# Two-layer trunk: x fetched ahead of a weight chunk, loads moved from GpSimd's queue to SP's, and a planner's costs retuned

## The chip, the cores and the metric

One NeuronCore of a Trainium2 chip runs the whole program. The metric is the device time of one execution in microseconds; 0.2% is about 2.1 us here. Engines are TensorE (PE, with its weight loads PEld), VectorE (DVE), ScalarE (ACT), GpSimd (POOL) and SyncE (SP); SP, ACT and POOL each issue DMAs on a queue of their own.

## The reference

x has 512 tokens of width 1024, in float32. Two layers, each a token mixer and a SwiGLU network with RMS norms before and after:

```python
for i in range(DEPTH):                 # DEPTH = 2
    h = rmsnorm(x, norm_mix_pre[i])
    m = swa_sink_attention(h, ...) if i % 2 == 0 else chunked_sgu(h, ...)
    x = x + rmsnorm(m, norm_mix_post[i])
    h = rmsnorm(x, norm_ffn_pre[i])
    x = x + rmsnorm(swiglu(h, ffn_w_gate_up[i], ffn_w_down[i]), norm_ffn_post[i])
```

The attention has 16 query heads on 4 key heads of width 64, rotary positions, a window of 128 tokens and a learned sink per head. The width of the SwiGLU networks is 2816. Everything this document speaks of lies in the first layer's attention and at its two ends.

## The kernel before, in words

**Products.** Every float32 operand is split into a rounded high part and the remaining low part, and a product is made of three products of TensorE (high x high, high x low, low x high; `mm3`, line 281). Weights come in chunks of 128x1024 (512 KB). For a chunk, ScalarE rounds the high part `wh` (line 360), and the low part `wl` = `raw` - `wh` comes from VectorE's subtraction (line 331) or, for the chunks in `BY_DMA`, from ScalarE writing -`wh` (line 352) and an adding DMA on GpSimd's queue (line 355).

**The order of the work.** The kernel is recorded by a planner in Python. It keeps estimated clocks, `now[0]` for TensorE and `busy` for VectorE, ScalarE, the DMA queue and GpSimd; side tasks are generators (`Side`), and each yields the time at which its next step is due by these estimates. While the main loop records TensorE's products, every step that is due is recorded too. The estimates (`mm`, `V`, `A`, `ROT`, `RSD`, `DMA_LOW` and so on) therefore set only the order in which instructions stand on each engine. On the chip each engine runs its instructions in that order, and each waits for its real operands.

**DMAs.** The semaphores of SP's and ScalarE's DMAs are eight, used in turn: each DMA waits until the one eight places before it has landed. SP's queue is therefore a list with at most eight in flight, and what stands at its head holds up all that follows. At the start stand, in this order, chunk 0 of the weights, the transposed x in four pieces `xg0` to `xg3` with chunk 1 between the last two, chunk 2, x itself in four pieces `x0` to `x3` (`load_x`, line 453, called when chunk `NLATE` is due), then chunk 3, masks, tables (`cs`) and chunk 4. Chunks in `POOL_LOAD` go over GpSimd's queue.

**The start.** TensorE is kept busy with products of zeros (line 243) until `WARM`. The value projection (`vproj`, 96 products of 256 columns, 64 with the high parts of chunks 0 and 1 and then 32 with their low parts) needs the transposed x. The RMS norm of the first layer is applied late: `rows_rms` (line 1470) squares x0 to x3, takes the root and, by a diagonal matrix and one product with ones (line 1502), spreads it as `rbc`, with which the projections are multiplied as they leave PSUM.

**The attention.** Ten projection tiles follow, two pairs of key heads with one key tile and four query tiles each; each tile is 24 products of 512 columns on one chunk (chunks 2 to 11). `evac_qk` (line 982) takes a tile out of PSUM (line 997, into an `rt` tile), rotates it with four DMAs on SP's queue (line 1003), then does three VectorE steps (lines 1006, 1008, 1009), a ScalarE step for the high part (line 1013) and a VectorE step for the low part (line 1016). The planner takes `ROT` for the four DMAs. Scores come in units of one pair of heads and 128 queries, two groups of twelve products per unit (line 1088); the first group's first six products use the key and query 0, its second six the key and query 1. Then follow VectorE's maximum (line 1093), ScalarE's exponentials, the division by the sum (lines 1116 to 1126: VectorE scales all but `NA` of four score tiles, ScalarE the rest), transposes (line 1159) and the products with the values (line 1151). TensorE's rows of projections and, later, of the output projection (lines 1261 and 1280) stand between these as fillers.

**The end of the attention.** Each token block's output is squared, scaled and added to x (`Tok`, lines 621 to 666); `NextH` (line 512) then makes the transposed, normalised input of the SwiGLU network in parts `hh` (line 605) and `hl` (line 609), the first two blocks by a product with a diagonal matrix (line 590).

Of the kernel before, what the change touches and what calls it, by code (L numbers as in the profile page):

```python
# [13 lines left out]
P = 128  # L14
# [9 lines left out]
MAGIC = 0x5F3759DF  # L24
NW = 19
NP = 2
PITCH = 0.107
DMA_LOW = 6.0
BY_DMA = (8, 10, 12, 13, 14, 15, 16, 17, 18, 19, 20, 21, 22)
ROT = 4.0  # L30
NY = 3
P0 = 3
NT = 3
# [7 lines left out]
DLAT = 1.7  # L41
X_0 = 4.9
RS = (0.27406385, -4.2420223, 5.2654107, -0.90349173, 1.7067959)
RSD = 1.4
NA = 1
SCALE = ("av", "av", "av", "av")
DIAG = (0, 1)
POOL_LOW = ()
POOL_LOAD = range(5, 16)
ALT = (1, 2, 3)  # L50
WARM = 8.0
ORDER = ("w", 0, 1, 2, "w", 3)
ACT_SQ = ()
NLATE = 3
GROUPS = ((0,), (1,), (2, 3))


# [96 lines left out]
def trunk_kernel(ctx, tc, x_t, xt, w, cols, rows, ws_t, consts, out):  # L154
    nc = tc.nc
# [43 lines left out]
    now = [0.0]  # L199
# [74 lines left out]
    def mm(ps, a, b, start, stop):  # L274
        nc.tensor.matmul(ps, a, b, start=start, stop=stop)  # L275
        n = 1
        for d in b.shape[1:]:
            n *= d
        now[0] += max(n * 0.000422, PITCH)

    def mm3(ps, ah, al, bh, bl, start, stop):
        mm(ps, ah, bh, start, False)
# [11 lines left out]
    def fetch(free=0.0, most=NBLK):  # L294
        while len(raws) < min(NCH, most):
            c = len(raws)
            n = len(STREAM[c][0])
            if raw_used[0] + n > NRAW[stage[0] in (2, 6)] or used[0] + raw_used[0] + n > NW:
                return
            if c == NLATE:  # L300
                load_x()
            if c == NLATE + 1:
                nc.sync.dma_start(c_msk[:, 0:256], consts[:, 1024:1280])
                nc.sync.dma_start(c_msk[:, 256:384], consts[:, 1408:1536])
                nc.sync.dma_start(cs[:], consts[:, 0:1024])
                busy["d"] += 2.5
            tiles = []
            for b in reversed(STREAM[c][0]):
                raw = wp.tile([P, CB * P], F32, tag="w", name=nm("raw"))
                (nc.gpsimd if c in POOL_LOAD else nc.sync).dma_start(raw[:], w[b])  # L310
                busy["d"] = max(busy["d"], now[0], free) + 1.46
                tiles.insert(0, raw)
            raw_used[0] += len(tiles)
            raws[c] = (tiles, busy["d"] + DLAT)
# [117 lines left out]
    c_id = cp.tile([P, P], F32, name="c_id")  # L432
# [3 lines left out]
    xg = [wp.tile([P, 2, S], F32, tag="w", name=f"xg{q}") for q in range(NB)]  # L436
    used[0] += NB
    nc.scalar.dma_start(c_cols[:], cols)
    first_act = sp.tile([P, 8], F32, tag="first", name="first", bufs=1)
    nc.vector.memset(first_act[:], 0.0)  # L440
    nc.scalar.activation(first_act[:], first_act[:], AF.Copy)
    nc.gpsimd.dma_start(c_id[:], consts[:, 1280:1408])
    nc.gpsimd.dma_start(c_row[:], rows[0:272].partition_broadcast(P))
    arrive = {}
    busy["d"] = X_0 - DLAT + 0.2 - 1.46
    for o in ORDER:
# [65 lines left out]
    class NextH:  # L512
# [57 lines left out]
        def turn(self, ts):  # L570
            if self.h is None:
                self.h = [[hp.tile([P, S], F32R, tag=t, name=nm(t)) for _ in range(KT)] for t in ("hh", "hl")]
            n = P * len(ts)
# [3 lines left out]
            for k0 in range(0, KT, kn):  # L577
# [7 lines left out]
                for k in range(k0, k0 + kn):  # L585
                    for i, t in enumerate(ts):
# [3 lines left out]
                            nc.tensor.matmul(dst, xs[t][:, k * P:(k + 1) * P], self.src[t], start=True, stop=True)  # L590
                        else:
                            nc.tensor.transpose(dst, self.src[t][k // 4][:, (k % 4) * P:(k % 4 + 1) * P], ident)  # L592
                        now[0] += 0.22 if self.diag(t) else 0.11
                if 1 in ts and k0 + kn == KT and self.dg is not None:
                    give("rt")
                Side(self.evac(ts, range(k0, k0 + kn), ps, now[0] + 0.2, alt), now[0] + 0.2, True)
# [375 lines left out]
    def attention(nx_in, g1o, nx_out):  # L972
# [132 lines left out]
        def softmax(u, g2, st, es, sm, f):  # L1105
# [9 lines left out]
            yield f  # L1115
            nc.vector.tensor_tensor(sm[:, jj], sm[:, jj], es[:, jj], ALU.add)
            nc.vector.reciprocal(sm[:, jj], sm[:, jj])
            V(4, f, 0.13)
            V(4, f, 0.15)
            f = busy["v"] + LAT  # L1120
            for j in js[NA:]:
                nc.vector.tensor_scalar(p(j), p(j), sm[:, j:j + 1], None, ALU.mult)
# [7 lines left out]
        def values(u):  # L1130
# [13 lines left out]
            def pv(kt):  # L1144
# [4 lines left out]
                for i in range(2):  # L1149
                    o = (2 * pr + i) * 64  # L1150
                    nc.tensor.matmul(po[i * 64:i * 64 + 64, :], vt[n - nkt + 1 + kt][:, o:o + 64], todo[2 * kt + i],  # L1151
                                     start=kt == 0, stop=kt == nkt - 1)
                    now[0] += 0.02 if i else 0.86
                    give("t")

            for z, (i, kt) in enumerate(groups):
# [462 lines left out]
```

## Time and profile before

| | |
|---|---|
| median of 3 runs | 1044.04 us (1043.73 to 1044.79) |
| the profiled execution | 1043.52 us |
| its span, first to last instruction | 1041.7 us |
| mean granted clock of TensorE | 0.995 |
| busy: PE, DVE, ACT, POOL | 1024.0, 665.8, 453.1, 35.3 us |

A line such as `PE acc L275 <- ACT ga L1013: 4.2, 1, 4.2` in the table of waits says who waited (engine, tile, line of the kernel), for whom, how long in total, how often and how long at most. A line of the timeline begins with start and duration in us; in brackets stands the engine's idle time before the instruction and what ended it. A line of the stretches gives, for each engine, the busy time and the number of instructions, then the granted clock, the DMA share and GB/s. A line of a group has, after its count, busy us and the mean in ns of one instruction, then the idle time before them. TensorE's products overlap, so what one costs is the distance from start to start, not its duration.

### The profile page before, as it was taken

The page shows a single profiled execution, that of the slowest core. Times are in us where ns is not written, and L with a number is a line of the kernel's source. Part 1 is how long each engine was busy: PE and PEld are TensorE (multiplying, and loading weights), DVE is VectorE, ACT ScalarE, POOL GpSimd, SP SyncE. Part 2 cuts the span into 40 slices and gives each one's busy share as a digit, 9 for nine tenths or more (in the row PEclk, how much of TensorE's full clock was granted, in tenths as well). Part 3 has the DMA queues.
Part 4 walks back from the last instruction along what each step waited for, and adds up shares of the span by engine and source line. Part 5 has one row for each costly group of instructions (what it writes and reads, how often), then busy time and mean ns, then how long its engine had stood idle before and what let it go on. Part 6 is the DMA issues. An engine that isn't in the chain of part 4 may idle for free.

```text
span 1041.7 us, 13505 instructions
## 1 busy us (share of the span) xinstructions
PE 1024.0 (98%) x5137; PEld 850.4 (82%) x5137; DVE 665.8 (64%) x1209; ACT 453.1 (43%) x791; POOL 35.3 (3%) x43
## 2 busy tenths in 40 slices
PE   8989999999999999999999999999999999999997
PEld 7766666988888888888889888899888888888886
DVE  5679877644445658778594967474344656787746
ACT  5349886532233333344264343563223334334421
POOL 1101002000000000000010000110000000000000
PEclk9989999999999999999999999999999999999999
DMA  9456555143435455554243332033444544555302
GB/s 349 116 147 162 133 139 165 42 133 130 162 131 190 144 162 184 208 173 161 83 142 104 99 126 78 24 139 122 146 137 168 196 142 156 187 198 186 123 20 81
DMA packets 42961, 148.11 MB, mean 142 GB/s; under 512 B 5344, under 2 KB 5856, under 8 KB 42896
## 3 DMA queue, kind: packets, MB, share of 16 engines
q1 hardware_dynamic: 38640, 133.52, 38.4%
q0 software_dynamic: 3536, 12.79, 5.4%
q8 instruction: 40, 0.66, 0.3%
q10 hardware_dynamic: 720, 0.94, 0.3%
q14 instruction: 25, 0.20, 0.1%
HBM read 135.69 MB, written 2.10 MB: 132 GB/s over the span
## 4 chain that ended last, share of the span: by engine, by line
PE 89%; DMA 4%; DVE 4%; ACT 1%; SPq 1%; issue 1%; DVEq 0%; ACTq 0%
PE acc L275 86%; DMA rt<-rt 2%; DMA raw<-w 1%; DMA x<-x_t 1%; PE acc L1151 1%; PE aux L1159 1%; SPq L1003 1%; PE aux L592 1%; DMA c_cols<-cols 0%; DVE rt L1006 0%; DVE rt L1008 0%; DVE p L1093 0%; DVE wl L331 0%; DVE rt L1009 0%; DVE rt L997 0%
## 5 line engine op out<-in xcount | busy, mean ns | idle before, releaser
L275 PE MATMUL acc<-hh,wh 128*128 128x512 f32 (+1 forms) x960 | 353.1, 368 | 0.0
L275 PE MATMUL acc<-hl,wh 128*128 128x512 f32 (+1 forms) x960 | 350.7, 365 | 2.1 <-DVE hl L609 2.1
L275 PE MATMUL acc<-hh,wl 128*128 128x512 f32 (+1 forms) x960 | 350.4, 365 | 0.0
L331 DVE TENSOR_TENSOR wl<-raw,wh 128x1024 fp32r<-128x1024 f32 x187 | 228.0, 1227 | 149.7 <-ACT wh L360 79.4
L275 PEld LDWEIGHTS acc<-hl,wh 128*128 128x128 f32 x960 | 181.7, 189 | 31.3 <-DVE hl L609 2.6
L275 PEld LDWEIGHTS acc<-hh,wh 128*128 128x128 f32 x960 | 181.6, 189 | 29.6 <-issue 0.2
L275 PEld LDWEIGHTS acc<-hh,wl 128*128 128x128 f32 x960 | 181.5, 189 | 28.9
L360 ACT ACTIVATE wh<-raw 128x1024 fp32r<-128x1024 f32 x160 | 165.7, 1052 | 90.6 <-PE acc L275 57.6
L275 PE MATMUL acc<-wh,rt 128*128 128x512 f32 x496 | 162.3, 389 | 0.0
L275 PE MATMUL acc<-wh,ga 128*128 128x512 f32 (+1 forms) x344 | 120.0, 396 | 0.0
L275 PEld LDWEIGHTS acc<-wh,rt 128*128 128x128 f32 x496 | 93.1, 188 | 19.4
L275 PE MATMUL acc<-wl,rt 128*128 128x512 f32 x248 | 96.5, 389 | 0.0
L891 DVE TENSOR_TENSOR m<-m,acc 128x512 f32<-128x512 f32 x80 | 51.9, 684 | 44.2 <-PE acc L275 32.9
L275 PEld LDWEIGHTS acc<-wh,ga 128*128 128x128 f32 x344 | 64.4, 188 | 18.6 <-issue 4.1
L275 PE MATMUL acc<-wl,ga 128*128 128x512 f32 (+1 forms) x206 | 79.1, 384 | 0.0
L338 ACT ACTIVATE wh<-raw 128x1024 fp32r<-128x1024 f32 x40 | 42.3, 1059 | 71.9 <-DVE raw L343 71.9
L869 ACT ACTIVATE rt<-t 128x512 fp32r<-128x512 f32 x40 | 25.3, 633 | 87.1 <-DVE t L864 68.9
L275 PEld LDWEIGHTS acc<-wl,rt 128*128 128x128 f32 x248 | 46.6, 188 | 9.6
L343 DVE TENSOR_TENSOR raw<-raw,raw 128x1024 f32<-128x1024 f32 x40 | 48.8, 1219 | 0.0
L778 ACT ACTIVATE t<-acc 128x512 f32<-128x512 f32 (+1 forms) x38 | 20.2, 531 | 59.6 <-PE acc L275 59.6
L636 POOL TENSOR_TENSOR m<-m,row 128x512 f32<-128x512 f32 x12 | 16.8, 1430 | 846.6 <-ACT acc L502 846.6
L275 PEld LDWEIGHTS acc<-wl,ga 128*128 128x128 f32 x206 | 38.8, 189 | 6.2
(151 smaller groups left out, 967.6 us busy)
## 6 DMA issues: line engine op xcount, KB each, us to landing
raw<-w SPq DMA_DIRECT2D x229, 512.0 KB, 3.5
wl<-raw POOLq DMA_DIRECT2D x13, 512.0 KB, 5.2
raw<-w POOLq DMA_DIRECT2D x11, 512.0 KB, 7.1
row<-rows SPq DMA_DIRECT2D x8, 512.0 KB, 4.8
rt<-rt SPq DMA_DIRECT2D x40, 64.0 KB, 3.0
xg<-xt SPq DMA_DIRECT2D x4, 512.0 KB, 8.5
x<-x_t SPq DMA_DIRECT2D x4, 512.0 KB, 13.4
out<-x SPq DMA_DIRECT2D x4, 256.0 KB, 2.1
```

The source lines that it names most:

```text
L275: nc.tensor.matmul(ps, a, b, start=start, stop=stop)
L331: nc.vector.tensor_tensor(wl[:], raw[:], wh[:].bitcast(F32), ALU.subtract)
L338: nc.scalar.activation(wh[:], raw[:], AF.Copy)
L343: nc.vector.tensor_tensor(raw[:], raw[:], tiles[1][:], op)
L360: nc.scalar.activation(wh[:], raw[:], AF.Copy)
L592: nc.tensor.transpose(dst, self.src[t][k // 4][:, (k % 4) * P:(k % 4 + 1) * P], ident)
L636: nc.gpsimd.tensor_tensor(self.m[c][:], self.m[c][:], self.g1[:, cols2[c]], ALU.mult)
L778: nc.scalar.activation(t1[:, hf], pg[:, hf], AF.Silu)
L869: nc.scalar.activation(hi, src, AF.Copy)
L891: nc.vector.tensor_tensor(d, d, ps[i][:], ALU.subtract if sign == "-" else ALU.add)
L1003: nc.sync.dma_start(ro[o:o + 32, hf], t1[q * 32:q * 32 + 32, hf])
L1151: nc.tensor.matmul(po[i * 64:i * 64 + 64, :], vt[n - nkt + 1 + kt][:, o:o + 64], todo[2 * kt + i], start=kt == 0, stop=kt == nkt - 1)
```

## The change

Line numbers after it are one lower, but for lines 302 to 437, which are the same. Its parts:

- `BY_DMA` loses chunks 8 and 10: their low parts come from VectorE's subtraction (line 331) instead of ScalarE's step and the adding DMA.
- `NLATE` 3 to 2: x0 to x3 stand ahead of chunk 2 on SP's queue, and chunk 3 and all behind it follow.
- `POOL_LOAD` 5..15 to 8..15: chunks 5, 6 and 7 go over SP's queue.
- `c_row` (value bias and sinks) goes from GpSimd's queue at the start to SP's queue behind chunk 2; the identity `c_id` goes from GpSimd's queue to ScalarE's.
- `NA` 1 to 0: VectorE scales all four score tiles of a group, ScalarE none.
- `WARM` 8.0 to 7.3: 34 products of zeros instead of 37.
- Estimates: `ROT` 4 to 6, `RSD` 1.4 to 1.0, the cost of a product by columns, of products with 64 rows, of transposes with a diagonal, of the reciprocal and of a values product.

```diff
-PITCH = 0.107
-BY_DMA = (8, 10, 12, 13, 14, 15, 16, 17, 18, 19, 20, 21, 22)
-ROT = 4.0
+BY_DMA = (12, 13, 14, 15, 16, 17, 18, 19, 20, 21, 22)
+ROT = 6.0
-RSD = 1.4
-NA = 1
+RSD = 1.0
+NA = 0
-POOL_LOAD = range(5, 16)
+POOL_LOAD = range(8, 16)
-WARM = 8.0
+WARM = 7.3
-NLATE = 3
+NLATE = 2
...
-        now[0] += max(n * 0.000422, PITCH)
+        now[0] += 0.058 if a.shape[0] == 64 else max(n * 0.0004168 + 0.0136, 0.112)
...
             if c == NLATE + 1:
+                nc.sync.dma_start(c_row[:], rows[0:272].partition_broadcast(P))
                 nc.sync.dma_start(c_msk[:, 0:256], consts[:, 1024:1280])
...
     nc.scalar.dma_start(c_cols[:], cols)
+    nc.scalar.dma_start(c_id[:], consts[:, 1280:1408])
...
-    nc.gpsimd.dma_start(c_id[:], consts[:, 1280:1408])
-    nc.gpsimd.dma_start(c_row[:], rows[0:272].partition_broadcast(P))
...
-                        now[0] += 0.22 if self.diag(t) else 0.11
+                        now[0] += 0.11
...
-            V(4, f, 0.13)
-            V(4, f, 0.15)
+            V(4, f, 0.18)
+            V(4, f, 0.2)
...
-                    now[0] += 0.02 if i else 0.86
+                    now[0] += 0.02 if i else 0.71
```

The order of the instructions changes on every engine through the attention. Three places matter for what follows. The first is the start of SP's queue; `raw_32` is chunk 2, `raw_35` chunk 3, `raw_40` chunk 4 before, and `raw_59`, `raw_63`, `raw_66`, `raw_71` are chunks 4 to 7 after. Before:

```order
L310 DMA raw_2_111<-w 128x1024
L450 DMA xg3_99<-xt 128x1024
L310 DMA raw_32_179<-w 128x1024
L455 DMA x0_87<-x_t 128x1024
L455 DMA x1_88<-x_t 128x1024
L455 DMA x2_89<-x_t 128x1024
L455 DMA x3_90<-x_t 128x1024
L310 DMA raw_35_241<-w 128x1024
L303 DMA c_msk_92<-consts 128x256
L304 DMA c_msk_92<-consts 128x128
L305 DMA cs_95<-consts 128x1024
L310 DMA raw_40_290<-w 128x1024
```

And after, from x on:

```order
L454 DMA x3_90<-x_t 128x1024
L310 DMA raw_32_182<-w 128x1024
L302 DMA c_row_94<-rows 128x272
L303 DMA c_msk_92<-consts 128x256
L304 DMA c_msk_92<-consts 128x128
L305 DMA cs_95<-consts 128x1024
L310 DMA raw_35_242<-w 128x1024
L310 DMA raw_59_358<-w 128x1024
L310 DMA raw_63_384<-w 128x1024
L310 DMA raw_66_399<-w 128x1024
L310 DMA raw_71_427<-w 128x1024
L1002 DMA rt_67_404<-rt_67_404 32x512 x4
```

Chunk 2 stands behind x0 to x3 now, c_row comes in, and the first rotation (`rt_67`) stands behind chunk 7.

The second place is VectorE's row around the rotation of query 1, the third tile (`rt_80` before, `rt_83` after; the key is `rt_66` or `rt_67`, query 0 `rt_74` or `rt_75`, query 2 `rt_87` or `rt_91`). Before:

```order
L331 TENSOR_TENSOR wl_78_473<-raw_71_433,wh_77_472 128x1024
L1006 SCALAR_TENSOR_TENSOR rt_74_447<-rt_74_447,c_cols_91,cs_95 128x512
L1008 SCALAR_TENSOR_TENSOR rt_74_447<-rt_74_447,c_cols_91,cs_95 128x512
L1009 TENSOR_TENSOR rt_74_447<-rt_74_447 128x512
L997 TENSOR_TENSOR rt_80_495<-acc_75_448,rbc_396 128x512
L1016 TENSOR_TENSOR ga_5_118<-rt_74_447,ga_4_117 128x512
L331 TENSOR_TENSOR wl_86_536<-raw_79_484,wh_85_535 128x1024
L997 TENSOR_TENSOR rt_87_538<-acc_81_496,rbc_396 128x512
L1006 SCALAR_TENSOR_TENSOR rt_80_495<-rt_80_495,c_cols_91,cs_95 128x512
```

After, where `wl_81` and `wl_89` are the low parts of chunks 8 and 10:

```order
L331 TENSOR_TENSOR wl_81_490<-raw_74_442,wh_80_489 128x1024
L996 TENSOR_TENSOR rt_83_495<-acc_76_448,rbc_366 128x512
L1005 SCALAR_TENSOR_TENSOR rt_75_447<-rt_75_447,c_cols_91,cs_95 128x512
L1007 SCALAR_TENSOR_TENSOR rt_75_447<-rt_75_447,c_cols_91,cs_95 128x512
L1008 TENSOR_TENSOR rt_75_447<-rt_75_447 128x512
L331 TENSOR_TENSOR wl_86_521<-raw_79_473,wh_85_520 128x1024
L1015 TENSOR_TENSOR ga_5_117<-rt_75_447,ga_4_116 128x512
L331 TENSOR_TENSOR wl_89_538<-raw_82_493,wh_88_537 128x1024
L996 TENSOR_TENSOR rt_91_543<-acc_84_496,rbc_366 128x512
L1005 SCALAR_TENSOR_TENSOR rt_83_495<-rt_83_495,c_cols_91,cs_95 128x512
```

The evacuation of query 1 has moved from behind the three steps of query 0 to ahead of them, and more stands between it and its own first step.

The third place is VectorE's row at the end of the attention, where the last four of eight `hl` pieces of the first two token blocks are made. Before (between `hl_337` and the first update of x3 stand the eight steps of a root):

```order
L642 TENSOR_TENSOR m_253_1615<-m_253_1615,row_254_1617 128x512
L609 SCALAR_TENSOR_TENSOR hl_336_1941<-aux_358_2008,c_cols_91,hh_328_1933 128x256
L609 SCALAR_TENSOR_TENSOR hl_337_1942<-aux_358_2008,c_cols_91,hh_329_1934 128x256
L508 SCALAR_TENSOR_TENSOR u_360_2036<-sq_310_1881 128x1
...
L655 SCALAR_TENSOR_TENSOR x3_90<-m_243_1552,rc_366_2043,x3_90 128x512
L655 SCALAR_TENSOR_TENSOR x3_90<-m_253_1615,rc_366_2043,x3_90 128x512
L609 SCALAR_TENSOR_TENSOR hl_338_1943<-aux_359_2017,c_cols_91,hh_330_1935 128x256
L609 SCALAR_TENSOR_TENSOR hl_339_1944<-aux_359_2017,c_cols_91,hh_331_1936 128x256
```

After:

```order
L331 TENSOR_TENSOR wl_356_1995<-raw_298_1818,wh_355_1994 128x1024
L608 SCALAR_TENSOR_TENSOR hl_333_1930<-aux_357_2000,c_cols_91,hh_325_1922 128x256
L608 SCALAR_TENSOR_TENSOR hl_334_1931<-aux_357_2000,c_cols_91,hh_326_1923 128x256
L608 SCALAR_TENSOR_TENSOR hl_335_1932<-aux_358_2008,c_cols_91,hh_327_1924 128x256
L608 SCALAR_TENSOR_TENSOR hl_336_1933<-aux_358_2008,c_cols_91,hh_328_1925 128x256
L331 TENSOR_TENSOR wl_363_2049<-raw_309_1870,wh_362_2048 128x1024
L641 TENSOR_TENSOR m_257_1599<-m_257_1599,row_258_1601 128x512
L507 SCALAR_TENSOR_TENSOR u_368_2083<-sq_310_1876 128x1
```

The last two pieces have moved ahead of the root and of the updates of x3; a chunk's low part stands ahead of the four.

## The prediction

> **What bounds the kernel now.** I read the page first, then TensorE's waits over the whole span, then the timeline and the stretches around the largest wait, and last the chain of waits that leads to it.
>
> ```profile
> span 1041.7 us, 13505 instructions
> PE 1024.0 (98%) x5137; PEld 850.4 (82%) x5137; DVE 665.8 (64%) x1209; ACT 453.1 (43%) x791; POOL 35.3 (3%) x43
> ...
> PE acc L275 <- ACT ga L1013: 4.2, 1, 4.2
> PE acc L275 <- DVE hl L609: 2.1, 2, 1.4
> ...
> PE aux L590 <- issue: 0.9, 1, 0.9
> PE aux L1159 <- ACT t L1163: 0.3, 1, 0.3
> ```
>
> TensorE is busy 98% of the span, so only two things can move the time: work of TensorE, which this change leaves alone but for three warming products, and TensorE's gaps, 17.7 us in all. The waits name the largest: one of 4.2 us for a rotated query (line 1013). Here it is on TensorE's timeline (start, duration), with the granted clock of the stretches around it (PEclk, third column from the right) and of the rest of the attention:
>
> ```profile
> 51.01 0.55 PE L275 MATMUL acc<-gb,ga 64*128 64x128 f32 x6
> 55.79 1.20 PE L275 MATMUL acc<-gb,ga 64*128 64x128 f32 x6 [4.22 <-ACT ga L1013]
> 56.92 0.79 PE L275 MATMUL acc<-hh,wh 128*128 128x512 f32 x1
> ...
> 61.35 0.42 PE L275 MATMUL acc<-hl,wh 128*128 128x512 f32 x1
> ...
> 54.00:55.00 1.00, 0.00 (x0) 0.00 (x0) 0.97 (x2) 0.00 (x0) 0.00 (x0) 0.78 0.90 348
> 55.00:61.00 6.00, 5.17 (x16) 4.00 (x17) 4.59 (x15) 3.20 (x11) 0.00 (x0) 0.50 0.50 153
> ...
> 62.00:174.00 112.00, 111.40 (x637) 77.77 (x635) 87.81 (x296) 88.48 (x238) 17.14 (x19) 1.00 0.58 140
> ```
>
> Half of the first scores run at 51.01, the other half at 55.79. After about 3 us of standing still the granted clock falls to 0.50. Six score products then take 1.13 us (55.79 to 56.92) instead of 0.55, and ten projection products 4.43 us (56.92 to 61.35) where ten at full clock take 2.27 (0.227 each, worked out below). The wait thus costs 4.22 + 0.58 + 2.16 = 7.0 us.
>
> The Trainium skill (TensorE: Matmul & The Clock Gate, Part 1: The HAM clock gate) gives about 3.4 us of standing still before the clock halves and about 3.4 us of work before it is back. Its fall agrees with the row; by its return the slow part would cost half of 3.4, 1.7 us, and the wait 5.9. The rows show some 6.5 us at half clock, so 7.0 stands.
>
> What TensorE waits for, on the chain of work (start, duration), and from the GpSimd queue's timeline:
>
> ```profile
> 46.22 0.61 DVE rt L997
> ...
> 48.67 4.14 DMA rt<-rt
> ...
> 52.93 0.75 DVE rt L1006
> ...
> 55.10 0.64 ACT ga L1013
> ...
> 48.27 0.89 POOL L355 DMA_DIRECT2D wl<-raw  x1 [13.53 <-ACT wl L352]
> ```
>
> The third rotation (query 1) leaves PSUM only at 46.22. Its four DMAs take until 52.93, 6.1 us after 46.83; the last meets the adding DMA of chunk 8, issued at 48.27. Three VectorE steps follow (52.93 to 55.10, 2.2 us) and ScalarE's high part (0.64).
>
> **The start.** ScalarE's first steps show when transfers land (they start on landing), TensorE's rows what they hold up:
>
> ```profile
> 9.03 1.34 ACT L1461 ACTIVATE hh<-xg,c_cols 128x512 fp32r<-128x512 f32 x2 [1.47 <-DMA xg<-xt]
> 11.80 1.34 ACT L1461 ACTIVATE hh<-xg,c_cols 128x512 fp32r<-128x512 f32 x2 [1.43 <-DMA xg<-xt]
> ...
> 14.52 1.34 ACT L1461 ACTIVATE hh<-xg,c_cols 128x512 fp32r<-128x512 f32 x2 [0.22 <-DMA xg<-xt]
> 15.80 1.06 ACT L360 ACTIVATE wh<-raw 128x1024 fp32r<-128x1024 f32 x1
> 17.08 0.64 ACT L1483 ACTIVATE j<-x 128x512 f32<-128x512 f32 x1 [0.22 <-DMA x<-x_t]
> ...
> 20.60 0.64 ACT L1483 ACTIVATE j<-x 128x512 f32<-128x512 f32 x1 [1.51 <-DMA x<-x_t]
> ...
> 22.82 0.63 ACT L1483 ACTIVATE j<-x 128x512 f32<-128x512 f32 x1 [1.50 <-DMA x<-x_t]
> ```
>
> ```profile
> 7.81 0.36 PE L275 MATMUL acc<-wh,hh 128*128 128x256 f32 x1
> ...
> 14.35 0.39 PE L275 MATMUL acc<-wh,hh 128*128 128x256 f32 x1 [1.69 <-ACT wh L360]
> ...
> 18.28 4.00 PE L275 MATMUL acc<-wl,hh 128*128 128x256 f32 x32
> 22.12 0.40 PE L275 MATMUL acc<-hh,wh 128*128 128x512 f32 x1
> ...
> 26.24 1.02 PE L1502 MATMUL aux<-rt,ones 128*128 128x512 f32 x2
> ...
> 27.34 0.40 PE L275 MATMUL acc<-hl,wh 128*128 128x512 f32 x1
> ...
> 50.69 0.39 PE L275 MATMUL acc<-hh,wl 128*128 128x512 f32 x1
> ```
>
> A 512 KB transfer takes 1.28 us when SP's queue is alone (14.52, 15.80, 17.08), 2.2 us (20.60 to 22.82) when chunks 6 and 7 come over GpSimd's queue beside it, and 2.8 us (9.03 to 11.80) with chunk 5 and c_row there. The change keeps that queue free until the value projection has ended. The products of the value projection take 0.12 us (32 of them from 18.28 to 22.12); 96 would take 11.5 us, and from 7.81 to 22.12 they took 14.3. So 2.8 us are waits, 1.69 of them for chunk 1. A projection product takes 0.227 us (103 from 27.34 to 50.69).
>
> After, in steps of 1.28 us from xg1's predecessor (about 6.2, one ScalarE pair, 1.34, and its idle 1.47 before 9.03): xg1 7.5, xg2 8.8, chunk 1 10.1, xg3 11.3, x0 to x3 12.6 to 16.5, chunk 2 17.7, c_row 18.1. Chunk 1's high part (1.06) is there at 11.2, before its first product (7.81 + 32 x 0.12 = 11.7), so 2.4 of the 2.8 us go; the rest I leave to VectorE's last low parts. Three warming products fewer are worth 0 to 0.5; I take 0.1. The value projection ends at 19.6. The product with ones comes 3.4 us after x3 (22.82 to 26.24): 19.9. With its neighbour it holds TensorE 1.1 us (26.24 to 27.34), 0.87 beyond that neighbour. The low part of chunk 2 (a 1.2 us VectorE step behind the diagonal and the nsink step, which now needs c_row) is there at 21.1, when the third product of the first tile needs it. So the projections start at 20.8 instead of 22.12 + 0.87 = 23.0: **-2.2 us**, between -2.8 and -0.5 (chunk 2 late by 1.7).
>
> **The first scores.** There stand 123 projection products ahead of them, before and after: the larger ROT does not move them on TensorE. What moves is VectorE's row: the evacuation of query 1 stood behind the three steps of query 0 and now stands ahead of them. Their DMAs meet loads on GpSimd's queue as before, but no adding DMA of chunk 8 or 10. Rotations, from evacuation to the step behind, first and slowest:
>
> ```profile
> 31.98 0.68 DVE L997 TENSOR_TENSOR rt<-acc,rbc 128x512 f32<-128x512 f32 x1
> ...
> 39.16 0.75 DVE L1006 SCALAR_TENSOR_TENSOR rt<-rt,c_cols,cs 128x512 f32<-128x512 f32 x1 [4.35 <-DMA rt<-rt]
> ...
> 64.11 0.70 DVE rt L997
> ...
> 67.61 5.97 DMA rt<-rt
> ```
>
> That is 6.5 us, and 8.8 us (64.81 to 73.58). After: the key's tile ends at 20.8 + 24 x 0.227 = 26.2, leaves by 26.9, is rotated by 33.4 (6.5) and through the three steps by 35.6. Two low parts (1.2 each), its own low part and query 1's evacuation (0.7 each) bring that to 39.4. With 6.1 us again it is rotated at 45.5, when VectorE has done its other 6.0 us (three steps, two low parts, two of 0.7). High part at 48.3, low part behind one more chunk at 49.6. The first six scores come at 51.01 - 2.2 = 48.8, the second six, which read query 1, at 49.3 and its low part at 49.7. The wait goes: **-6.7 us**, leaving 0.3 for so thin a margin. Next late would be the same low part. With 8.8 us for both rotations the wait is 4.0 us and the clock falls again: -0.2 is the other bound. Rotations stay behind chunks 4 to 7 on SP's queue; query 0's four DMAs wait for exactly those to land. Behind c_row come six transfers of 512 KB and two small ones: at 1.28 us each they end near 26, at 2.2 near 32, when query 0's tile ends too (20.8 + 48 x 0.227 = 31.7). That is hidden, barely in the second case.
>
> **VectorE's added work.** Steps and means in the attention:
>
> ```profile
> L1122 DVE TENSOR_SCALAR p<-p,sm 128x256 f32<-128x256 f32 (+1 forms) x36 | 9.9, 333 | 0.4
> L331 DVE TENSOR_TENSOR wl<-raw,wh 128x1024 fp32r<-128x1024 f32 x8 | 9.8, 1220 | 3.3 <-ACT wh L360 3.3
> ...
> L1126 ACT ACTIVATE p<-p,sm 128x256 f32<-128x256 f32 (+1 forms) x12 | 5.6, 463 | 0.7 <-DVE sm L1117 0.5
> ```
>
> Sixteen scalings, one of four in two groups of eight units, come from ScalarE (12 of them in this row) to VectorE (0.333 each, 5.3 us), and two low parts (2.4 us). VectorE has 24 us free from 62 to 174 and TensorE waited there only 0.3 us, for a link of the same chain; I double that: **+0.6 us**, between 0 and 5.3. Two ScalarE copies and two adding DMAs go, at nothing, since nothing waits for them but the rotation above.
>
> **The end of the attention.** The longer of the two waits for hl is for its last pieces:
>
> ```profile
> 186.69 0.87 DVE L609 SCALAR_TENSOR_TENSOR hl<-aux,c_cols,hh 128x256 fp32r<-128x256 f32 x2
> ```
>
> These stood behind the last token's chain and now stand ahead of it, behind one chunk. Of 1.4 us I take **-1.0 us**, between -2.1 (both waits) and 0 (a step behind becomes late); the 0.9 us stay. The retuned costs of one product change little else: TensorE's waits, asked for the first 200 us alone, are the same rows, so the rest has none to lose.
>
> **The sum.** -2.2 - 6.7 + 0.6 - 1.0 = -9.3. The profiled execution took 1043.5 us (span 1041.7), 0.5 below the median: 1034.2 + 0.5 = **1034.7 us**. All bounds at their best give -2.8 - 7.0 - 2.1 = -11.9, 1032.1.
>
> **Rivals.**
> - *A rotation is late again* (the first scores, or a later one: 8.8 us is on record). For: the margin is under 1 us. Against: no adding DMA beside it. A wait of 2 to 4 us, with or without the halved clock: 1037 to 1041.5. Chance 0.21.
> - *SP's queue stays at 2.2 us a transfer.* x3 lands at 6.2 + 8 x 2.2 = 23.8, chunk 2 at 26.0, its low part (1.06 + 1.2) at 28.3; TensorE stands from 19.6 and the clock halves: the projections start 5.3 us later instead of 2.2 earlier, with up to 2.1 more for the clock, and the rest gives 7.1 back: 1042 to 1044. Against: GpSimd's queue is empty then. Chance 0.05.
> - *VectorE becomes the bound of the attention* (the slower case). While TensorE stood and crawled, VectorE caught up; if it sets the stage, the 7.0 us are no gain and 7.7 us come on top: 1044.0 - 2.2 + 7.7 = 1049.5. It decides once VectorE has no idle left; from 62 to 174 it is busy 87.81 of 112 us, 78%. Chance 0.05.
> - *The added scalings hold back GpSimd's queue.* Eleven adding DMAs remain; each late by one more scaling (0.333) is 3.7 us if TensorE waits for all: 1038.4. Against: none of TensorE's waits names a weight's low part from such a DMA. Chance 0.03. By the Trainium skill (SBUF — State Buffer, SBUF: two separate sides) a VectorE step that uses both read ports keeps GpSimd from writing its DMA descriptors; no run here shows it.
> - The change not doing what it says: the order has both subtractions on VectorE, so none.
>
> **Chances.** The forecast has 0.66, from 1031.8 to 1037. The range 1031.8 to 1041 leaves out the slower case and parts of two rivals. About 0.2% (2.1 us) is what a measurement of this kernel can tell from no change: faster 0.88 (the forecast, nearly all of the late rotation, the scalings), same 0.07 (SP's slow queue and what is left of a late rotation), slower 0.05.
>
> **What would show it.** Right: chunk 1's wait gone and the first projection at about 20.8; the first scores at about 49 in one piece with the clock at 1.00 from 50 to 62; the last hl pieces without a wait. Wrong: a wait for line 1012's ScalarE step with a clock of 0.50 behind it, a wait for chunk 2 near 20, or new waits between 75 and 145 behind VectorE's scalings.

## The result and the profile after

The changed kernel takes 1037.27 us (median of 4 runs, 1037.13 to 1037.39), the kernel before 1043.9 us (1043.73 to 1044.79) on the same chip: a ratio of 0.9934, with a 95% interval of 0.9923 to 0.9946. That is 6.6 us faster where 9.3 were forecast; the time lies 2.6 us above the 1034.7 of the forecast, inside the range (1031.8 to 1041) and 0.3 us outside the 1031.8 to 1037 that the forecast itself was given. The profiled execution took 1037.27 us (before 1043.52).

The page of the changed kernel, and then TensorE's largest waits over the span (who waited, for whom, total, times, longest):

```profile
span 1035.5 us, 13502 instructions
...
PE 1019.8 (98%) x5134; PEld 847.8 (82%) x5134; DVE 669.7 (65%) x1227; ACT 447.1 (43%) x773; POOL 30.3 (3%) x36
```

```profile
PE aux L591 <- ACT m L557: 2.9, 5, 1.3
PE aux L1158 <- ACT t L1162: 2.0, 2, 1.0
PE aux L589 <- issue: 1.7, 1, 1.7
```

The waits that the change aimed at are gone: chunk 1's (1.7), the rotated query's (4.2) and the two for hl (2.1). Three others are longer or new, and the largest stands in no row of before: transposes (line 591) that wait five times for ScalarE's line 557. It lies behind 500 us, in a part that the prediction gave no term. There `NextH` makes the input of the next network: the root of each token block's mean square (nine small VectorE steps from line 542 on), then x times the root, half by VectorE (line 560), half by ScalarE (line 557), then the transposes.

**The first 60 us went as forecast.** TensorE's timeline of the changed kernel (start, duration): the ones product, the third projection product, the twelve first scores and the two products that answer to 56.92 and 61.35 of before:

```profile
19.52 1.10 PE L1501 MATMUL aux<-rt,ones 128*128 128x512 f32 x2 [0.20 <-DVE rt L1497]
...
21.32 0.50 PE L274 MATMUL acc<-hh,wl 128*128 128x512 f32 x1 [0.24 <-DVE wl L331]
...
48.97 0.89 PE L274 MATMUL acc<-gb,ga 64*128 64x128 f32 x12
49.78 0.50 PE L274 MATMUL acc<-hh,wh 128*128 128x512 f32 x1
...
52.16 0.39 PE L274 MATMUL acc<-hl,wh 128*128 128x512 f32 x1
```

The stretch that stood at half clock before:

```profile
55.00:61.00 6.00, 6.00 (x28) 4.96 (x27) 4.80 (x8) 3.82 (x5) 1.41 (x2) 1.00 0.79 201
```

The first scores begin at 48.97 instead of 51.01, all twelve in one piece, and the clock stays at 1.00. The eleventh product behind them stands at 52.16, before at 61.35: 9.2 us earlier.

**Where the rest went.** The same VectorE steps in both kernels show how far the whole is ahead. First before: the first step of a root near 520, the update of x near 667. Then the same steps after:

```profile
524.72 0.16 DVE L543 SCALAR_TENSOR_TENSOR u<-s 128x2 f32<-128x2 f32 x1 [0.19 <-ACT m L502]
...
667.50 1.41 DVE L655 SCALAR_TENSOR_TENSOR x<-m,rc,x 128x512 f32<-128x512 f32 x2
```

```profile
514.29 0.16 DVE L542 SCALAR_TENSOR_TENSOR u<-s 128x2 f32<-128x2 f32 x1 [0.19 <-ACT m L501]
...
658.96 1.42 DVE L654 SCALAR_TENSOR_TENSOR x<-m,rc,x 128x512 f32<-128x512 f32 x2
```

And TensorE's last product, before and after:

```profile
1034.36 0.28 PE L275 MATMUL acc<-wh,gb 128*128 128x256 f32 x1
```

```profile
1027.89 0.28 PE L274 MATMUL acc<-wh,gb 128*128 128x256 f32 x1
```

The changed kernel is 10.4 us ahead at 514, more than forecast, 8.5 at 659, and 6.5 at the end. It gained 10.4 us in the first 200 us and lost 3.9 at the two places where the next network's input is made. The first of these places on TensorE, before and after:

```profile
528.59 0.60 PE L592 MATMUL aux<-c_id,m 128*128 128x128 f32 x4
```

```profile
515.90 0.39 PE L274 MATMUL acc<-wh,gb 128*128 128x512 f32 x1
517.56 0.33 PE L591 MATMUL aux<-c_id,m 128*128 128x128 f32 x1 [1.28 <-ACT m L557]
518.18 0.55 PE L591 MATMUL aux<-c_id,m 128*128 128x128 f32 x3 [0.28 <-ACT m L557]
```

ScalarE's scaling in the kernel before:

```profile
527.21 1.34 ACT L558 ACTIVATE m<-x,rc 128x512 f32<-128x512 f32 x2 [1.91 <-DVE rc L497]
```

Before, that pair ended at 528.55, 0.04 us ahead of the transposes, which began 3.87 us behind the root's first step (524.72 to 528.59) and did not wait; nothing was spare. After, TensorE arrives at about 516.1, 1.8 us behind that step (514.29), and stands. In TensorE's row the transposes have moved ahead of nine products; nine products of 0.227 us are the 2.0 us. The root takes 2.4 us here in both kernels (514.29 to 516.69 after), because one of its steps takes 1.21 us beside a scaling on GpSimd (last section); the planner took it as 1.7 before and as 1.3 after, which fits a root that is not held (165.13 to 166.47 in `lo_pool`) and not this one.

### The profile page after: what moved, and what is told of

It reads as the page before. It is cut to its first block, busy times and chain, and to the rows that moved or that the text cites. A ratio compares the mean times of both kernels' runs of the same rounds, so it can differ in the third digit from the quotient of the medians.

```text
span 1035.5 us, 13502 instructions
## 1 busy us (share of the span) xinstructions
PE 1019.8 (98%) x5134; PEld 847.8 (82%) x5134; DVE 669.7 (65%) x1227; ACT 447.1 (43%) x773; POOL 30.3 (3%) x36
## 4 chain that ended last, share of the span: by engine, by line
PE 92%; ACT 3%; DVE 2%; DMA 2%; issue 0%; SPq 0%; DVEq 0%; ACTq 0%
PE acc L274 89%; PE acc L1150 1%; PE aux L1158 1%; DMA raw<-w 1%; PE aux L591 1%; DMA xg<-xt 1%; ACT m L501 0%; ACT m L557 0%; ACT p L1112 0%; PE aux L589 0%; DVE wl L331 0%; ACT wh L360 0%; DVE x L654 0%; ACT acc L501 0%; DVE m L641 0%
```

## Theories

*Order*: the two retuned estimates that hold beyond the attention, a root (`RSD` 1.4 to 1.0) and a product (0.216 to 0.227 us for 512 columns), make the planner call for the transposes too early. A shorter root makes them due sooner, and a longer product puts fewer products into the same estimated time. In the order of the instructions the root's estimate alone moves the first transposes ahead of 6 products, the product's alone of 3, both of 9; no run times the two apart. *Chain* (rival): the root and the scaling themselves come later in the changed kernel, so that any order would wait.

For the first scores there were two candidates as well: the place of query 1's evacuation in VectorE's row, or the adding DMA of chunk 8 that runs beside its rotation. The later runs take the best kernel so far, `late_old`, and undo or move one thing each.

## The experiments

| kernel | median us | ratio to before, 95% interval |
|---|---|---|
| late_old | 1033.26 | 0.9892 (0.9878 to 0.9905) |
| late_new | 1048.18 | 1.0036 (1.0023 to 1.0048) |
| start_only | 1047.19 | 1.0028 (1.0018 to 1.0039) |
| rot_only | 1050.27 | 1.0055 (1.0042 to 1.0067) |
| lo_bydma | 1042.52 | 0.9983 (0.9974 to 0.9991) |
| lo_rot4 | 1038.91 | 0.9943 (0.9929 to 0.9956) |
| lo_na1 | 1040.66 | 0.9961 (0.9949 to 0.9973) |
| lo_mmold | 1038.08 | 0.9939 (0.9927 to 0.9950) |
| lo_diag | 1037.63 | 0.9937 (0.9925 to 0.9950) |
| lo_pool | 1036.54 | 0.9924 (0.9911 to 0.9938) |
| lo_neg | 1036.43 | 0.9923 (0.9910 to 0.9935) |
| lo_rsd | 1035.46 | 0.9913 (0.9899 to 0.9927) |

The kernel before ran beside them at medians of 1044.35 to 1044.59 us.

### late_old and late_new: the estimates behind the attention

`late_old` is the changed kernel with

```diff
-        now[0] += 0.058 if a.shape[0] == 64 else max(n * 0.0004168 + 0.0136, 0.112)
+        now[0] += (0.058 if a.shape[0] == 64 else max(n * 0.0004168 + 0.0136, 0.112)) if stage[0] < 3 else max(n * 0.000422, 0.107)
...
-        busy["v"] = max(busy["v"], ready) + RSD + 0.1 * len(us)
+        busy["v"] = max(busy["v"], ready) + (RSD if stage[0] < 3 else 1.4) + 0.1 * len(us)
```

> The changed kernel with the planner's old estimates (a root at 1.4, a product at 0.216) from the second half of the first SwiGLU network on; the order up to there is the changed kernel's. Theory (order): the 3.95 us that the changed kernel loses again behind 500 us come from the new estimates, which put the transposes of the normalised input 9, 3 and 15 products further forward than before, in front of ScalarE's scaling. Then the five waits of the transposes for line 557 go and the time is 1037.3 - 3.95 = 1033.3 us. Rival (chain): the roots and scalings themselves come later in the changed kernel, whatever the order; then the time stays at 1037.3.

Measured: 1033.26 us, the best of all. TensorE at the first of the two places, in `late_old`:

```profile
517.83 0.39 PE L274 MATMUL acc<-wh,gb 128*128 128x512 f32 x1
518.06 0.60 PE L591 MATMUL aux<-c_id,m 128*128 128x128 f32 x4
...
1023.87 0.28 PE L274 MATMUL acc<-wh,gb 128*128 128x256 f32 x1
```

The transposes stand 9 products further back and wait for nothing; the last product starts 10.5 us earlier than before (1034.36), so that nothing is lost any more. From 200 us on `late_old` has no row of waits at all.

`late_new` is the opposite edit on the kernel before: the new estimates from stage 3 on.

```diff
-        now[0] += max(n * 0.000422, PITCH)
+        now[0] += max(n * 0.000422, PITCH) if stage[0] < 3 else 0.058 if a.shape[0] == 64 else max(n * 0.0004168 + 0.0136, 0.112)
...
-        busy["v"] = max(busy["v"], ready) + RSD + 0.1 * len(us)
+        busy["v"] = max(busy["v"], ready) + (RSD if stage[0] < 3 else 1.0) + 0.1 * len(us)
```

> The kernel before with the two new estimates only from the second half of the first SwiGLU network on. Theory (order): the same waits appear, 1.87 us at about 527 and 0.6 + 1.5 us behind 665, and the time is 1043.9 + 3.95 = 1047.9 us. Rival (chain): no wait, 1043.9.

Measured: 1048.18 us, 3.6 more than before, with the same wait in `late_new`'s table:

```profile
PE aux L592 <- ACT m L558: 2.9, 5, 1.3
```

Both directions agree: the order theory holds, the rival falls.

### start_only and rot_only: one part alone

`start_only` gives the kernel before the new start alone:

```diff
-POOL_LOAD = range(5, 16)
+POOL_LOAD = range(8, 16)
-WARM = 8.0
+WARM = 7.3
-NLATE = 3
+NLATE = 2
...
+                nc.sync.dma_start(c_row[:], rows[0:272].partition_broadcast(P))
...
+    nc.scalar.dma_start(c_id[:], consts[:, 1280:1408])
...
-    nc.gpsimd.dma_start(c_id[:], consts[:, 1280:1408])
-    nc.gpsimd.dma_start(c_row[:], rows[0:272].partition_broadcast(P))
```

> The kernel before with only the start changed (x ahead of chunk 2, chunks 5 to 7, c_row and c_id off GpSimd's queue, three products of zeros fewer); ROT, the low parts of chunks 8 and 10 and all other estimates as before. The start itself is worth 2.0 us by both theories. Theory (order on VectorE): the wait of the first scores comes from the place of query 1's evacuation behind the three steps of query 0; with this edit it stands ahead of them, without the larger ROT, so the wait of 7 us goes too: 1034.7, between 1034 and 1036. Rival (adding DMA): the rotation of query 1 still meets chunk 8's adding DMA, the wait stays: 1041.9.

Measured: 1047.19 us, slower than before and outside both. VectorE's timeline in `start_only`: the four evacuations of the value projection, chunk 2's low part, the evacuation of query 1 and the first step behind its rotation:

```profile
19.95 1.65 DVE L1058 SCALAR_TENSOR_TENSOR vt<-acc,rc,c_row 128x256 f32<-128x256 f32 x4
21.53 1.21 DVE L332 TENSOR_TENSOR wl<-raw,wh 128x1024 fp32r<-128x1024 f32 x1
...
39.19 0.68 DVE L997 TENSOR_TENSOR rt<-acc,rbc 128x512 f32<-128x512 f32 x1
...
50.47 0.75 DVE L1006 SCALAR_TENSOR_TENSOR rt<-rt,c_cols,cs 128x512 f32<-128x512 f32 x1 [2.70 <-DMA rt<-rt]
```

GpSimd's queue in `start_only` at that time:

```profile
39.96 0.89 POOL L356 DMA_DIRECT2D wl<-raw  x1 [9.19 <-ACT wl L353]
```

Two things failed. The old order has the 1.65 us of evacuations ahead of chunk 2's low part, and TensorE waits 1.5 us for it, so that of the start's 2.0 us only 0.5 are left. And though query 1 is evacuated at 39.19, 7 us earlier than before (46.22), its rotation takes 10.6 us (39.87 to 50.47) beside the adding DMA that GpSimd issued at 39.96; the wait of the first scores stays (3.7 us). The evacuation ahead of query 0's steps is thus not enough by itself here. Counted by TensorE's products, `start_only` is level with the kernel before at 62 us; the 3.3 us that its profiled execution is behind at the end come later, 2.2 of them between 175 and 190, and no run takes them apart.

`rot_only` is the kernel before with

```diff
-ROT = 4.0
+ROT = 6.0
```

> The kernel before with ROT 6.0 alone. The evacuation of query 1 stands ahead of the three steps of query 0; the adding DMAs of chunks 8 and 10 stay, the start is as before. Theory (order on VectorE): the wait of 4.2 us goes with its half clock, -7.0: 1036.9. Rival (adding DMA): the rotation is still held up by chunk 8's adding DMA, the gain is at most the few tenths by which it begins earlier: 1042 to 1044.

Measured: 1050.27 us. At the first scores this gained: twelve scores with a wait of 0.2 us between, since query 1's evacuation is at 42.91 there, and that with chunk 8's adding DMA still in place: it was issued at 45.01, behind three of the rotation's four DMAs, and the rotation took 6.8 us (43.59 to 50.39). But the whole attention is put in another order, and at its end TensorE stood for the diagonal, in `rot_only`:

```profile
180.88 3.78 PE L590 MATMUL aux<-rt,x 128*128 128x128 f32 x16 [6.76 <-DVE rt L552]
```

So the larger ROT does help the first scores, and by itself it costs more at the end than it brings.

### lo_bydma and lo_rot4: what keeps the first scores in one piece

```diff
-BY_DMA = (12, 13, 14, 15, 16, 17, 18, 19, 20, 21, 22)
+BY_DMA = (8, 10, 12, 13, 14, 15, 16, 17, 18, 19, 20, 21, 22)
```

> The kernel late_old (1033.3) with the low parts of chunks 8 and 10 made by the adding DMA again; ROT stays at 6, and query 1's evacuation still stands ahead of the three steps of query 0. Theory (adding DMA, from start_only, where query 1's four DMAs took 9.4 us beside chunk 8's adding DMA): the rotation of query 1 takes over 8 us again and the wait of the first scores returns, 3 to 4 us with its half clock behind it: 1038 to 1041. Rival (order on VectorE): the evacuation is early enough, so the wait stays away: 1033 to 1034.

Measured: 1042.52 us, 9.3 more than `late_old` and above the theory's 1041. VectorE in `lo_bydma`, then GpSimd's queue and TensorE there:

```profile
37.86 0.68 DVE L996 TENSOR_TENSOR rt<-acc,rbc 128x512 f32<-128x512 f32 x1
...
49.06 0.75 DVE L1005 SCALAR_TENSOR_TENSOR rt<-rt,c_cols,cs 128x512 f32<-128x512 f32 x1 [5.43 <-DMA rt<-rt]
```

```profile
38.12 0.89 POOL L355 DMA_DIRECT2D wl<-raw  x1 [8.86 <-ACT wl L352]
38.68 1.41 POOL L310 DMA_DIRECT2D raw<-w  x2
```

```profile
51.91 0.44 PE L274 MATMUL acc<-gb,ga 64*128 64x128 f32 x4 [3.10 <-ACT ga L1012]
```

GpSimd's queue stands 8.86 us for ScalarE's negative high part, then issues the adding DMA and the two loads held up behind it at once. The rotation beside them takes 10.5 us (38.54 to 49.06). In the changed kernel, with a load here and there on that queue, query 1 is evacuated later and its first step finds the rotation done:

```profile
38.60 0.68 DVE L996 TENSOR_TENSOR rt<-acc,rbc 128x512 f32<-128x512 f32 x1
...
44.73 0.74 DVE L1005 SCALAR_TENSOR_TENSOR rt<-rt,c_cols,cs 128x512 f32<-128x512 f32 x1
```

So what GpSimd's queue moves at that time is a cause. Which part of that traffic it is stays open: the adding DMA landed 6.4 us after its issue, at about 44.5, the two loads at 46.3 and 48.8, and the rotation ended with the second load; no run has the adding DMA without these loads. And the moment counts: here and in `start_only` the adding DMA was issued ahead of all four of query 1's DMAs and the rotation took 10.5 and 10.6 us, while in the kernel before and in `rot_only` it came behind three of them and the rotation took 6.1 and 6.8. In the profiled execution (1044.71 us, the slowest of eleven) some 5.4 us are lost at the first scores, and some 5.7 more behind a wait of 2.3 us that ends at 102.9 (last section).

```diff
-ROT = 6.0
+ROT = 4.0
```

> The kernel late_old (1033.3) with ROT 4.0. Query 0's evacuation now stands behind the three steps of the key, query 1's still ahead of those of query 0. Theory (adding DMA): with nothing but loads beside it, each rotation takes 4 to 6 us, query 1 is rotated by about 44.5 and its high part there by 47.5, before the first scores at 49: 1033.3, up to 1034. Rival (the larger ROT is needed): query 1 comes 3 to 4 us later and the wait of up to 7 us returns: 1037 to 1040.

Measured: 1038.91 us, 5.6 more than `late_old`; the rival was right. The first scores stand for 2.86 us, in `lo_rot4`:

```profile
50.54 1.20 PE L274 MATMUL acc<-gb,ga 64*128 64x128 f32 x6 [2.86 <-ACT ga L1012]
```

Not for a slow transfer: query 1's DMAs end before 45, but VectorE reaches its first step only at 47.69. Query 0's evacuation is at 36.28 there, behind the steps of the key, instead of 32.08; everything after it on VectorE comes later, and a chunk's low part at 46.54 stands ahead of query 1's steps. With the new start both parts are needed, the one for the transfer, the other for VectorE's row; with the old start `ROT` alone took the wait away (`rot_only`).

### lo_na1, lo_mmold, lo_neg: the attention's own estimates

```diff
-NA = 0
+NA = 1
```

> The kernel late_old (1033.3) with NA 1: one of four scalings on ScalarE again. Theory (ScalarE's place): the two waits of the transposes in the attention, 2.0 us, are for ScalarE's negative high part (line 352), which stands ahead of a copy; VectorE's sixteen added scalings cost nothing by themselves, and with NA 1 waits of this size stay or move: 1032.5 to 1035. Rival (VectorE's added work): the scalings are what the 1.7 us more in the attention come from; without them the time falls by that: 1031.6.

Measured: 1040.66 us, 7.4 more than `late_old`; both expectations were too good. In `lo_na1` TensorE stands for one of the scalings that ScalarE has again:

```profile
96.29 0.88 PE L1158 MATMUL aux<-c_id,pm 128*128 128x128 f32 x6 [2.85 <-ACT pm L1125]
```

With the lower clock behind it (0.81 from 96 to 105) this costs about 4 us, and the rest comes at the attention's end. The rival's gain did not come. As `NA` also gives the attention another order, the run prices the setting as a whole, not VectorE's scalings alone.

```diff
-        now[0] += (0.058 if a.shape[0] == 64 else max(n * 0.0004168 + 0.0136, 0.112)) if stage[0] < 3 else max(n * 0.000422, 0.107)
+        now[0] += max(n * 0.000422, 0.107)
```

> The kernel late_old (1033.3) with the old estimate of a product throughout. In VectorE's row the four evacuations of the value projection (1.65 us) then stand ahead of chunk 2's low part, as in start_only. Theory (the estimate counts at the start): TensorE waits 1.5 us at about 22 for that low part, and the projections start at 22.4: 1034.8, with what the order of the attention's end adds or takes up to 1037. Rival (the retuned costs change little, as the prediction had it): 1033.3.

Measured: 1038.08 us, 4.8 more than `late_old`, above what was expected. The wait at the start is there (1.2 us for line 331), some 2 us go near 97 and some 3.5 at the attention's end, where hl is waited for again (1.8). So the same estimate that costs 3.9 us behind 500 us, together with the root's, is worth 4.8 us in front.

`lo_neg` takes chunks 15 and 18 from `BY_DMA`.

```diff
-BY_DMA = (12, 13, 14, 15, 16, 17, 18, 19, 20, 21, 22)
+BY_DMA = (12, 13, 14, 16, 17, 19, 20, 21, 22)
```

> The kernel late_old (1033.3) with the low parts of chunks 15 and 18 from VectorE instead of ScalarE's negative high part and the adding DMA. Theory (ScalarE's place): the two waits of the transposes for line 1162, 1.0 us each behind 94 and 139, come from these chunks' negative high parts standing ahead of the copy; they go, and TensorE has no wait over 0.5 us from 62 to 160. As the order of the attention is made anew from about 66 us on, other waits may come in: 1031.3, up to 1036. Rival (the copies are late for another reason): the same two waits stay.

Measured: 1036.43 us. What it was to show stands in the changed kernel's ScalarE row:

```profile
93.23 1.04 ACT L352 ACTIVATE wl<-wh 128x1024 fp32r<-128x1024 f32 x1
94.18 1.06 ACT L1162 ACTIVATE t<-aux 128x512 f32<-128x512 f32 x2
```

TensorE's transposes wait at 94.81 for that copy, which waited for a negative high part of 1.04 us. In `lo_neg` the one at 138.64 is gone and so is its wait; the one at 93.24 belongs to another chunk than I took, and its wait of 0.9 stays. The time lies 0.4 us above the expected 1036: the 3 us by which it is slower than `late_old` come at the end of the attention, by waits for the diagonal (2.2 us in all, 1.7 in `late_old`) with a granted clock of 0.50 behind them.

### lo_diag, lo_pool, lo_rsd: the last wait of the attention

`late_old` still waits 1.7 us for the diagonal. Three edits went for it, one each. The first:

```diff
-                    f = max(f, V(P // 2, 0, 0.13))
+                    f = max(f, V(P // 2, 0, 0.13)) + 1.5
```

> The kernel late_old (1033.3) in which the planner takes the diagonal of the first two token blocks as ready 1.5 us later, so that the eight products with it stand 9 products (2.0 us) further back on TensorE. Nothing ahead of them moves. Theory (order): the diagonal is late by 1.7 us for the place of these products only; the wait goes and nothing behind it is late: 1031.6. Rival (chain): the parts of the next input, which hang on these products, come 2 us later in the row, and the wait moves to the first products that read them: 1033.3 or more.

In `lo_pool` the second entry of `PLAN` has `(1,)` in place of `(1, 2)`, the blocks that GpSimd scales at the attention's end:

```diff
-(6.0, 0.8, 0.0, (3,), (1, 2))
+(6.0, 0.8, 0.0, (3,), (1,))
```

> The kernel late_old (1033.3) with the two scalings of token block 2 at the end of the attention on VectorE instead of GpSimd. Theory (GpSimd holds VectorE): in the changed kernel a VectorE step of 0.16 us takes 1.19 and a pair of 1.42 takes 2.28 where they begin inside a GpSimd scaling of 1.29, and they end with it; without these two scalings both go back to 0.16 and 1.42, the diagonal comes 1.9 us earlier and the wait of 1.7 us goes: 1031.6, up to 1033 for VectorE's two steps of 0.69. Rival (the long steps have another cause): they stay long, and the time is 1033.3 or more.

And `lo_rsd`:

```diff
-        busy["v"] = max(busy["v"], ready) + (RSD if stage[0] < 3 else 1.4) + 0.1 * len(us)
+        busy["v"] = max(busy["v"], ready) + 1.4 + 0.1 * len(us)
```

> The kernel late_old (1033.3) with the old estimate of a root (1.4) throughout; the new estimate of a product stays up to the second half of the first SwiGLU network. The products with the diagonal at the attention's end stand 6 products (1.4 us) further back. Theory (the parts hold each other, from lo_diag and lo_pool): their wait falls from 1.7 to 0.3 us, but the parts of the next input come later in the row and waits for line 608 take its place, 2 to 4 us: 1034 to 1037. Rival (the shorter root is of no use anywhere): the wait goes and nothing takes its place: 1031.9.

Measured: 1037.63, 1036.54 and 1035.46 us, all slower than `late_old`. The largest waits from 150 to 200 us in `lo_diag`, in `lo_pool` and in `lo_rsd`, there with the one for the diagonal (line 589); in `lo_pool` 0.2 us of that are left, in `lo_diag` none:

```profile
PE acc L274 <- ACT hh L604: 2.4, 1, 2.4
PE acc L274 <- DVE hl L608: 1.8, 2, 1.1
```

```profile
PE acc L274 <- DVE hl L608: 3.0, 2, 1.5
```

```profile
PE acc L274 <- DVE hl L608: 2.4, 2, 1.5
...
PE aux L589 <- issue: 0.3, 1, 0.3
```

Each took most or all of the wait for the diagonal away, and each got back more: TensorE now waits for `hh` and `hl`, the next network's parts, which are made from these products. In `lo_diag` the rival was right. In `lo_pool` VectorE's steps did become short again (last section), so that its theory had the mechanism right and the price wrong. `lo_rsd` came out as its theory had it (0.3 and 2.4 us). Here the early place with its wait is the better one, the reverse of the places behind 500 us.

## Why the prediction was right, and where it was wrong

| step | forecast us | measured us | from |
|---|---|---|---|
| the start | -2.2 | -2.0 | 51.01 to 48.97 |
| the first scores | -6.7 | -7.2 | 61.35 to 52.16, less the start |
| VectorE's added work and the end of the attention | +0.6 - 1.0 | -1.2 | -9.2 to -10.4 |
| behind 200 us | 0 | +3.9 | -10.4 to -6.5 |
| sum | -9.3 | -6.5 | last product |

- **The start**: right in size and in its parts. The ones product stands at 19.52 (forecast 19.9), the third product at 21.32 (21.1 for the low part). Chunk 2 came later than forecast (its high part started at 18.95, not 17.7) and still cost only 0.24. But that depended on VectorE's order: `start_only` and `lo_mmold` wait 1.5 and 1.2 us where the evacuations stand ahead of chunk 2's low part. The prediction read the low part's place from the changed order without naming the estimate that set it.
- **The first scores**: right, with 0.5 us more than forecast. Query 1 was evacuated by 39.3 (forecast 39.4), and the rotation was not on the path at all: its first step at 44.73 waits for nothing. The price of the wait, worked out from the rows as 7.0, fits. By the quicker return of the clock in the Trainium skill (TensorE: Matmul & The Clock Gate, Part 1: The HAM clock gate) it would be an estimated 5.9; the runs show both, 6.9 us at half clock in the kernel before and 3.5 in `lo_na1`. Of the stated reason, `lo_bydma` shows the first half (no adding DMA beside it), for the adding DMA together with the loads behind it. The second half (the evacuation ahead of query 0's steps) is not enough: it stands so in `start_only` and `lo_rot4` too, and TensorE waits 3.7 and 2.9 us there. What the larger `ROT` adds in the changed kernel is query 0's evacuation ahead of the key's steps, at 32.08 instead of 36.28.
- **VectorE's added work**: the +0.6 was for VectorE. New waits did come at 94 and 139, where the prediction looked for them, 2.0 us (0.3 before); but they are for ScalarE, whose negative high part stands ahead of a copy. `lo_neg` shows this for the one at 139, the rows alone for the one at 94. `NA` 1, with the order that it brings, costs 7.4 us.
- **The end of the attention**: the two waits for hl (2.1) went, that for the diagonal grew from 0.9 to 1.7: -1.3 against -1.0. The 1.6 us that remain to the -1.2 of the table (1.7 - 1.3 is +0.4) come without a wait, from another order of products of several kinds; what part of the order does it was not tested.
- **The step that failed** is one sentence: the retuned costs of one product "change little else: TensorE's waits, asked for the first 200 us alone, are the same rows, so the rest has none to lose". That the rest had no wait to lose was true; that it had none to gain did not follow. The new root and product estimates reach every later place at which a step is due, and cost 3.9 us at two of them. The sum was off by that (+3.9) and by gains of 1.1 us that were not counted. That the time still lies in the range is in part luck: it lies where a late rotation had been given room, and none was late.
- **The rivals** did not come: no rotation was late, SP's queue kept its step of about 1.3 us but for chunk 2, VectorE set no stage, and no wait names a low part that an adding DMA made. `lo_bydma` and `lo_rot4` show that the first one was near.

## What to carry to other kernels

A planner's estimate acts wherever it is used: before forecasting, follow each retuned number to every place in the order that moves, and compare the moved instruction's new distance from its operand's last step with the old one. A stage without a wait says only that there is nothing to gain; how much it can lose must be read from that distance (here 2.0 us were moved where next to nothing was spare). And where parts were fitted together, one alone can lose what all of them win: the start alone and ROT alone were both slower than before.

## What the runs showed of the hardware

**GpSimd holds VectorE.** In the changed kernel, VectorE's steps and GpSimd's scalings (lines 654, 490 and 635):

```profile
160.90 2.28 DVE L654 SCALAR_TENSOR_TENSOR x<-m,rc,x 128x512 f32<-128x512 f32 x2
...
164.75 1.19 DVE L490 SCALAR_TENSOR_TENSOR vq<-vt 128x2 f32<-128x2 f32 x1
```

```profile
160.67 1.29 POOL L635 TENSOR_TENSOR m<-m,row 128x512 f32<-128x512 f32 x1 [1.36 <-ACT acc L501]
...
164.63 1.29 POOL L635 TENSOR_TENSOR m<-m,row 128x512 f32<-128x512 f32 x1 [1.83 <-ACT acc L501]
```

The step of 1.19 ends at 165.94, GpSimd's scaling at 165.92; such a step takes 0.16 elsewhere. Without these two scalings the same two rows of `lo_pool` read:

```profile
161.12 1.42 DVE L654 SCALAR_TENSOR_TENSOR x<-m,rc,x 128x512 f32<-128x512 f32 x2
...
165.92 0.16 DVE L490 SCALAR_TENSOR_TENSOR vq<-vt 128x2 f32<-128x2 f32 x1
```

The Trainium skill (SBUF — State Buffer, SBUF: two separate sides) says that the two engines share a pair of ports under an exclusive lock, so that of a VectorE step with two inputs in SBUF and a GpSimd instruction that reads SBUF the later one stands until the other has ended; the trace agrees, to 0.02 us. In the root's chain this adds up to 1.0 us where a scaling falls into it, before and after alike (1.21 us for such a step at 525.51 before and at 515.09 after).

**A wait's price is not set by its length alone.** Stretches of `lo_bydma` behind a wait of 2.3 us that ended at 102.9, of `lo_pool` behind one of 1.5 us that ended at 171.2, and in `lo_neg` a wait of 1.42 us with a stretch behind it (the granted clock is the third column from the right):

```profile
102.90:104.00 1.10, 1.07 (x8) 0.62 (x8) 1.10 (x6) 0.84 (x2) 0.00 (x0) 1.00 0.95 276
104.00:105.00 1.00, 1.00 (x5) 0.26 (x2) 0.96 (x6) 1.00 (x3) 0.00 (x0) 0.62 0.90 270
105.00:106.00 1.00, 1.00 (x6) 0.67 (x7) 0.93 (x5) 1.00 (x3) 0.00 (x0) 0.50 0.93 238
```

```profile
172.00:173.00 1.00, 1.00 (x12) 1.00 (x10) 1.00 (x3) 1.00 (x3) 0.00 (x0) 1.00 0.04 16
```

```profile
168.25 1.03 PE L589 MATMUL aux<-rt,x 128*128 128x128 f32 x4 [1.42 <-DVE rt L551]
...
169.00:170.00 1.00, 1.00 (x6) 0.90 (x5) 0.41 (x1) 0.81 (x3) 0.00 (x0) 0.50 0.68 123
```

The waits of 1.5 us in `lo_pool` and of 1.7 us in the changed kernel left the clock at 1.00 and cost their own length. Behind the wait of 2.3 us it fell to 0.50, though only some 1.3 us after TensorE had begun again, and stayed there for 6.9 us; that wait cost some 5.7 us, its length and half of the 6.9. Every wait of 2.3 us or more in these runs was followed by 0.50. Of the shorter ones two were: the 1.42 us in `lo_neg`, with one of 0.77 us just ahead of it, and 1.78 us in `lo_mmold` (172.54 to 174.32). The clock stayed at 0.50 for about 3.5 us in `lo_na1`, `lo_diag` and `lo_neg`, 6.9 in the kernel before and in `lo_rot4`, and 10.3 in `rot_only`; what decides between them is open. The Trainium skill (TensorE: Matmul & The Clock Gate, Part 1: The HAM clock gate) gives about 3.4 us of standing still; here less was enough, and the measurement decides.
